# A transformer block on one core: both feed-forward products by seven block products in place of eight

## The chip, the core and the metric

The kernel runs on one core of one Trainium2 chip. The metric is device time in microseconds (us) of one execution; a time stated for a kernel is the median of its runs. Engines are named as the profile names them: PE is the matrix engine (PEld its weight loads), DVE the vector engine, ACT the scalar engine, POOL the GpSimd engine, SP the engine that issues most transfers. "L79" is line 79 of the kernel, the one helper through which almost every instruction of the four compute engines is recorded, so instructions are told apart by the tiles they write and read.

## What is computed

One block of a network on a sequence of 512 positions of width 2048, all in fp32: four token mixers on a joint projection, an output projection, and a feed-forward part with a squared ReLU. `N(v, w)` is `v * rsqrt(mean(v*v) + 1e-6) * w`.

```
h    = N(x, norm_mix_pre)
proj = h @ w_in                                    # 2048 x 6152
mix  = concat(hgrn2(..), gated_delta(..), spatial_gating(..), conformer_conv(..))
x    = x + N(mix @ w_out, norm_mix_post)           # 2048 x 2048
h    = N(x, norm_ff_pre)
y    = square(relu(h @ w_ff1)) @ w_ff2             # 2048 x 8192, 8192 x 2048
out  = x + N(y, norm_ff_post)
```

## The kernel before

**Precision.** The large products run in the `float32r` type. Each operand is split into a high part (`wh`, `xH`, `yH`) and the rest (`wl`, `xL`, `yL`), and a product is three matmuls into one PSUM bank: high with high, high with low, low with high (`mm3`, L405). Every matmul loads its own 128 x 128 stationary operand.

**Weights.** One stream (`Stream`, L355 and on) carries all weights in pieces of 512 KB. SP loads a piece into `raw` (three buffers, L365), ACT copies it to `wh`, DVE subtracts and writes `wl` (four buffers each). `plan` lists the pieces in the order in which PE uses them. A piece of `w_ff1` is 128 partitions of 4 KB in a row; a piece of `w_ff2` is two rows of 2 KB per partition.

**Order.** The program is written out for each engine by `Driver`: the main stream is a generator of matmuls, and tasks are woken by its estimate of time. Each engine's queue then runs in the order written, and an instruction that waits holds back those behind it. PSUM has two banks of kind `pj` and six of kind `mx`.

**Stages.** The projections and mixers run first; `out_job` (two halves of the tokens) multiplies by `w_out`, `x2_tail` adds the residual, stores it to DRAM (`x2d`) and writes the normalised rows, transposed and split, into the resident tile `R`. The feed-forward part follows. Its first products (`split_job`, L1477) take half of the tokens at a time, 256 columns per matmul, while the tails of the other half still run; `extras` has prepared two of its four blocks of weights early. Then eight rounds: eight blocks of 128 hidden features (`proj_F`, L413: stationary weights, all 512 tokens as columns), each squared after ReLU and split into `yH` and `yL` in SBUF (`relu2`); then `ff2_job`, which multiplies these by 1024 rows of `w_ff2` (stationary activations, 512 columns of weights) and adds the sum into `acc` in SBUF (`acc_add`). The last round (`ff2_last`) takes the tokens one group after the other for the last columns and finishes each group with `final`: row statistics, residual from `x2d`, four or five stores (L1613).

Of the kernel before, what the change touches and what calls it, by code (L numbers as in the profile page):

```python
# [12 lines left out]
F32 = mybir.dt.float32  # L13
# [55 lines left out]
class Eng:  # L69
    """An engine whose instructions also advance the driver's estimate of when it is free."""  # L70
# [51 lines left out]
class Driver:  # L122
    """Interleaves the instruction streams of many generators around one main stream of matmuls.

    A generator yields ("pe", banks) before matmuls that read what it has just computed, an Event to
    wait for it, or ("bg",) to go on only when the vector engine has nothing else to do.
    """
# [118 lines left out]
    def idle(self):  # L246
        """Nothing else to do: move on to the time at which some task is due."""
# [5 lines left out]
    def main(self, gen):  # L253
        """Run the main stream's generator, feeding tasks in between."""
# [32 lines left out]
def hybrid_trunk(ctx: ExitStack, tc: tile.TileContext, a, out):  # L287
# [117 lines left out]
    def mm3(o, aH, aL, bH, bL, first, last):  # L405
        T.matmul(out=o, lhsT=aH, rhs=bH, start=first, stop=False)
        yield PE0
        T.matmul(out=o, lhsT=aH, rhs=bL, start=False, stop=False)
        yield PE0
        T.matmul(out=o, lhsT=aL, rhs=bH, start=False, stop=last)  # L410
        yield PE0
# [947 lines left out]
    def x2_tail(t, yw, ss, evs, fin):  # L1359
# [33 lines left out]
        yield from to_R(t // 2, (t % 2) * P, yw, "mx", pre, hev[t])  # L1393

    hev = [[Event() for _ in range(4)] for _ in range(NT)]
# [47 lines left out]
    FB, SPLIT = 8, 4  # L1443
    NB = DFF // P // FB
    w1, w2 = a['w_ff1'], a['w_ff2']
    for b in range(NB):
        for j in range(FB):
            if b > 0 or j < 2 or j >= SPLIT:
                plan_F(w1, b * FB + j)
        for c in range(4):  # L1450
            plan.extend((rows2(w2, b * FB + 2 * i, c * 512), 2, 512) for i in range(FB // 2))

    extra = {}
    es_x = ExitStack()

    def extras():
        es_mix.close()
        px = es_x.enter_context(tc.tile_pool(name="px", bufs=1, reuse_waits="tile", side="right"))
        for e in range(2 * (SPLIT - 2)):
            j, kh = 2 + e // 2, e % 2  # L1460
            raw = p2.tile([P, 8, P], F32, tag="rawx", name="rawx", bufs=1)
            nc.sync.dma_start(out=raw, in_=w1[j, :, kh * 8:(kh + 1) * 8, :])
            drv.cur.time = drv.dma(1 << 19)
            yield ("bg",)
            h, l = (px.tile([P, 8, P], F32R, name=f"wx{e}{i}") for i in range(2))
            S.copy(out=h, in_=raw)
            V.tensor_tensor(out=l, in0=raw, in1=h.bitcast(F32), op=ALU.subtract)
            extra[j, kh] = (h, l, None)
            yield ("bg",)

    drv.main(out_job(0))
    exe = drv.spawn(extras())
    drv.main(out_job(1))

    heads = [Event() for _ in range(SPLIT)]

    def split_job():  # L1477
        yield exe
        yield ("pe", 2, "pj")
        bs = [Bank("pj") for _ in range(2)]  # L1480
        us = dict(extra)
        for hf in range(2):
            for j in range(SPLIT):
                if hf == 0 and j >= 2:
                    yield PE1
                    bs.append(Bank())
                for kh in range(2):
                    if hf == 0 and j < 2:
                        us[j, kh] = yield from st.get()
                    wh, wl, uid = us[j, kh]  # L1490
                    for kk in range(8):
                        k = kh * 8 + kk
                        for t in (2 * hf, 2 * hf + 1):
                            yield hev[t][k // 4]
                        yield from mm3(bs[j].t[:, hf * 256:(hf + 1) * 256], wh[:, kk, :], wl[:, kk, :],
                                       R[:, hf, 0, k, :], R[:, hf, 1, k, :], k == 0, k == KT - 1)
                    if hf == 1 and j < 2:
                        st.done(uid)
                if hf == 1:
                    heads[j].fire(drv.pe + 0.15, bs[j])  # L1500

    drv.main(split_job())
    es2.close()
    es_x.close()
    p3 = ctx.enter_context(tc.tile_pool(name="p3", bufs=1, reuse_waits="tile"))
    yH = p3.tile([P, FB, SEQ], F32R, name="yH")
    yL = p3.tile([P, FB, SEQ], F32R, name="yL")
    acc = p3.tile([P, NT, D], F32, name="acc")
    wfp = p3.tile([P, D], F32, name="wfp")
    yev = {}  # L1510

    def relu2(ev, j):
        yield ev
        r = p3.tile([P, 512], F32, tag="r", name="r", bufs=2)
        y2 = p3.tile([P, 512], F32, tag="y2", name="y2", bufs=2)
        S.activation(out=r, in_=ev.val.t, func=AF.Relu)
        ev.val.free()
        S.activation(out=y2, in_=r, func=AF.Square)
        yield PE0
        V.tensor_tensor(out=yH[:, j, :], in0=r, in1=r, op=ALU.mult)  # L1520
        V.tensor_tensor(out=yL[:, j, :], in0=y2, in1=yH[:, j, :].bitcast(F32), op=ALU.subtract)

    def ff2_mms(o, t, k, wh, wl):
        yh, yl = yH[:, k, t * P:(t + 1) * P], yL[:, k, t * P:(t + 1) * P]
# [211 lines left out]
```

## Time and profile before

| | us |
|---|---|
| median of 3 runs | 2278.02 |
| lowest and highest | 2276.43, 2278.62 |
| span of the profiled execution, first to last instruction | 2273.2 |

The page of the profile gives the busy time of each engine, the span in 40 slices, the chain of work that ended last, the costliest groups of instructions and the DMA issues. The trace behind it also answers for single stretches: the busy time of every engine, the granted clock of PE, the share of the 16 DMA engines' time that packets took, and GB/s. The share can come out a little over one, since packets on one engine overlap. Times of single PE instructions overlap as well, so the pace of PE is read from how many matmuls a piece of the chain holds.

### The profile page before, as it was taken

Reading aid. Unit: us, or ns where it says so; the run is one execution under the profiler, and the core shown is the slowest. Engines: PE = TensorE matmul, PEld = TensorE weight load, DVE = VectorE, ACT = ScalarE, POOL = GpSimd, SP = SyncE. Lnnn points to the kernel's source line nnn. Section 1 sums busy time; section 2 is a strip of 40 time slices with the busy share of each in tenths; the row PEclk is TensorE's granted clock in tenths of the full one; section 3 lists DMA queues with packets and bytes.
Section 4 is the critical chain, followed back from the end, with each engine's and each line's share of the span. In section 5 each row is a group of like instructions: output and inputs, shape, how many; then the busy total and the mean of one; then the engine's idle time right before and its main releaser. Section 6 shows DMA issues by size and latency. Waiting matters only on the chain.

```text
span 2273.2 us, 25758 instructions
## 1 busy us (share of the span) xinstructions
PE 2241.5 (99%) x10393; PEld 1848.3 (81%) x10393; DVE 1063.1 (47%) x1494; ACT 786.7 (35%) x1157; POOL 150.5 (7%) x186
## 2 busy tenths in 40 slices
PE   9899999999999999999999999999999999999998
PEld 7788888888888789888888888888888888888886
DVE  4656666877765764333333333333333333333335
ACT  6354444555554553212212212212212222322222
POOL 0231011211110000000000000000000000000013
PEclk9999999999999999999999999999999999999999
DMA  8232222222237772333332323333332333233334
GB/s 299 70 93 79 82 81 65 84 84 75 84 105 262 235 246 90 100 93 99 96 93 93 102 93 93 102 93 93 93 102 93 96 98 95 93 96 93 98 131 137
DMA packets 101750, 250.62 MB, mean 110 GB/s; under 512 B 8688, under 2 KB 11264, under 8 KB 100864
## 3 DMA queue, kind: packets, MB, share of 16 engines
q1 hardware_dynamic: 99184, 244.79, 34.0%
q10 hardware_dynamic: 2448, 4.20, 0.5%
q8 instruction: 81, 1.33, 0.2%
q14 instruction: 37, 0.30, 0.0%
HBM read 240.56 MB, written 8.40 MB: 110 GB/s over the span
## 4 chain that ended last, share of the span: by engine, by line
PE 90%; DMA 3%; DVE 3%; ACT 2%; issue 1%; POOL 1%; SPq 0%; DVEq 0%; ACTq 0%; POOLq 0%
PE pj L79 47%; PE mx L79 43%; DVE wl L79 1%; ACT wh L79 1%; DVE xT L79 1%; DMA raw<-in_w_cv_dram 0%; DMA rawx<-in_w_ff_dram 0%; ACT L79 0%; DMA rsd<-rs 0%; DMA wpost<-in_w_mix_post_dram 0%; DMA raw<-in_w_out_dram 0%; DMA x<-x2d 0%; DMA xT<-in_x_t_dram 0%; DMA rows<-in_rows_dram 0%; DMA xt<-in_x_dram 0%
## 5 line engine op out<-in xcount | busy, mean ns | idle before, releaser
L79 PE MATMUL pj<-R,wh 128*128 128x512 f32 (+1 forms) x3328 | 1033.1, 389 | 0.0
L79 DVE TENSOR_TENSOR wl<-raw,wh 128x1024 fp32r<-128x1024 f32 (+1 forms) x413 | 509.9, 1236 | 1025.1 <-ACT wh L79 1022.8
L79 ACT CAST wh<-raw 128x1024 fp32r<-128x1024 f32 (+1 forms) x413 | 430.5, 1044 | 896.3 <-PE mx L79 454.9
L79 PEld LDWEIGHTS pj<-R,wh 128*128 128x128 f32 x3328 | 618.4, 188 | 119.5
L79 PE MATMUL pj<-R,wl 128*128 128x512 f32 (+1 forms) x1664 | 646.8, 389 | 0.0
L79 PE MATMUL mx<-wh,yL 128*128 128x512 f32 (+1 forms) x1032 | 405.9, 393 | 0.5 <-DVE acc L79 0.5
L79 PE MATMUL mx<-wl,yH 128*128 128x512 f32 (+1 forms) x1032 | 405.9, 393 | 0.0
L79 PE MATMUL mx<-wh,yH 128*128 128x512 f32 (+1 forms) x1032 | 405.8, 393 | 0.0
L79 PEld LDWEIGHTS pj<-R,wl 128*128 128x128 f32 x1664 | 313.0, 188 | 59.2
L79 PE MATMUL mx<-wh,R 128*128 128x512 f32 x768 | 242.0, 395 | 6.9 <-ACT wh L79 6.9
L79 PEld LDWEIGHTS mx<-wh,yL 128*128 128x128 f32 x1032 | 193.4, 187 | 47.3 <-DVE acc L79 0.7
L79 PEld LDWEIGHTS mx<-wl,yH 128*128 128x128 f32 x1032 | 193.4, 187 | 47.1 <-DVE wl L79 0.5
L79 PEld LDWEIGHTS mx<-wh,yH 128*128 128x128 f32 x1032 | 193.4, 187 | 46.6
L79 PEld LDWEIGHTS mx<-wh,R 128*128 128x128 f32 x768 | 145.8, 190 | 37.6 <-ACT wh L79 7.3
L79 PE MATMUL mx<-wl,R 128*128 128x512 f32 x384 | 152.2, 396 | 2.3 <-DVE wl L79 1.5
L79 ACT ACTIVATE r<-pj 128x512 f32<-128x512 f32 x62 | 37.1, 598 | 278.6 <-PE pj L79 276.8
L79 POOL TENSOR_TENSOR acc<-acc,wfp 128x512 f32<-128x512 f32 x15 | 22.3, 1511 | 1376.7 <-ACT y L79 1376.7
L79 DVE TENSOR_TENSOR acc<-mx,acc 128x512 f32<-128x512 f32 (+1 forms) x113 | 77.6, 687 | 36.4 <-PE mx L79 35.6
L79 DVE SCALAR_TENSOR_TENSOR mix<-dy,cols,mix 128x512 f32<-128x512 f32 x120 | 92.5, 771 | 0.4
L79 PEld LDWEIGHTS mx<-wl,R 128*128 128x128 f32 x384 | 72.9, 190 | 18.8 <-DVE wl L79 4.0
L79 ACT ACT_TABLE_LOAD x54 | 69.3, 1283 | 7.2 <-DVE X L79 3.4
L79 DVE TENSOR_TENSOR yL<-y,yH 128x512 fp32r<-128x512 f32 x64 | 44.3, 692 | 4.5 <-ACT y L79 2.1
(248 smaller groups left out, 1142.6 us busy)
## 6 DMA issues: line engine op xcount, KB each, us to landing
raw<-in_w_ff_dram SPq DMA_DIRECT2D x252, 512.0 KB, 3.6
raw<-in_w_f_dram SPq DMA_DIRECT2D x80, 512.0 KB, 3.7
raw<-in_w_out_dram SPq DMA_DIRECT2D x64, 512.0 KB, 4.3
xt<-in_x_dram SPq DMA_DIRECT2D x8, 512.0 KB, 7.6
raw<-in_w_ai_dram SPq DMA_DIRECT2D x8, 512.0 KB, 4.4
x<-in_x_dram SPq DMA_DIRECT2D x16, 256.0 KB, 6.5
x2d<-x ACTq DMA_DIRECT2D x16, 256.0 KB, 3.9
out_dram<-x SPq DMA_DIRECT2D x15, 256.0 KB, 2.2
```

Source lines behind the costliest of these rows:

```text
L79: r = f(*args, **kw)
```

## The change

Both feed-forward products are cut into 2 x 2 blocks and computed by the seven products of Strassen's scheme in Winograd's form. For `h @ w_ff1`, the tokens are halved (256 and 256), the 2048 inputs (eight tiles of 128 each) and the hidden features (32 blocks of 128 each); a unit `u` is one pair of hidden blocks, 32 units. For `y @ w_ff2`, the units are eight rounds (four hidden blocks of each half, 512 rows) by two columns of 512 of each half, 16 units. A unit has products numbered 1 to 7, and three of them (2, 4, 3) go on in the bank of another (1, 7, 5).

- Sums of activations: `to_S` computes, for the second half of the tokens, the operands `S6`, `S7` and part of `R`; `s4_job` makes `S3`.
- Sums of weights: a buffer `X`, `V` (`raw`) or `W` is loaded by SP, and further blocks are added to it in place by transfers of POOL with `accum_op=ALU.add`. `X` holds one sum after the other: it is split for product 7, gets another block added, is split for 6, again for 4. `mill` splits the sums as the stream did (ACT, then DVE).
- Thirteen units (`HEAD`) have products 1 and 2, which need the first half of the tokens alone, computed ahead (`head_job`); the results go to DRAM (`stash`) and come back in `setup1`.
- Hidden activations: after products 6, 4 and 3 of a unit `evac1` forms the four blocks, applies ReLU and the square, forms the seven operands of the second scheme, splits them and stores both parts to DRAM (`ydr`, 0.92 MB each). `load_y` brings them back into the room of `R`, 1 MB for each round and product, in rows of 1 KB.
- The second product's results add up in five SBUF tiles (`accu`, `accg`, `accp`, `accc`, `accd`) in `evac2`; `final` works on them in place. The residual rows for it are loaded ahead.

```diff
-    FB, SPLIT = 8, 4
-    NB = DFF // P // FB
+    NU1, NU2, HEAD = 32, 16, 13
+    heads = [(u, p) for j in range(HEAD + 1) for u, p in ((j, 1), (j - 1, 2)) if 0 <= u < HEAD]
...
+    def unit_bufs(blk, head, xtag):
...
+            B["V", i] = Buf("V", [[b11, b12]] if head else [[b11], [b12]])
+            B["X", i] = Buf(xtag, [[b12, b22], [b11], [b21]])
+            B["W", i] = None if head else Buf("W", [[b21]])
+            B["Z", i] = Buf("W", [[b22]])
+        where = {1: ("V", 0), 5: ("V", 0 if head else 1), 7: ("X", 0), 6: ("X", 1), 4: ("X", 2), 2: ("W", 0), 3: ("Z", 0)}
...
+        late = [(u - 1, 4), (u - 1, 3)] if u else []
+        if head:
+            seq2 += [(u, 7), (u, 5)] + late + [(u, 6)]
+        else:
+            seq2 += [(u, 1), (u, 7)] + late + [(u, 5), (u, 2), (u, 6)]
...
+    def add_in(buf, stage, srcs):
+        for i, src in enumerate(srcs):
+            yield PE0
+            G.dma_start(out=buf.t, in_=src, accum_op=ALU.add)
...
+    def mill():
+        for j, (buf, stage) in enumerate(order):
+            i = base0 + j
+            yield st.room[i]
+            yield buf.ready[stage]
...
+            split((h, l), buf.t)
...
+            if stage + 1 < len(buf.stages):
+                drv.spawn(add_in(buf, stage + 1, buf.stages[stage + 1]), at=drv.cur.time)
+            else:
+                buf.free.fire(drv.cur.time)
...
-    drv.main(split_job())
...
+    drv.main(head_job())
+    drv.drain(tail + hdone)
     es2.close()
...
+    xr = ctx.enter_context(tc.tile_pool(name="xr", bufs=1, reuse_waits="tile"))
+    pools["X"], pools["W"] = (xr, "X", 2), (xr, "W", 2)
...
+    for tag in ("V", "X", "W"):
+        drv.spawn(loader(tag))
+    drv.spawn(mill())
...
+    def evac1(u, p, ev):
...
+        elif p == 6:
+            V.tensor_tensor(out=u2, in0=bt, in1=p1, op=ALU.add)
+            b.free()
+            V.tensor_tensor(out=yt[:, 2, :], in0=banks[u, 7][0].t[:, 0:256], in1=u2, op=ALU.add)
+            mid[u, 7].fire(drv.cur.time)
+            V.tensor_tensor(out=yt[:, 2, :], in0=banks[u, 5][0].t[:, 0:256], in1=yt[:, 2, :], op=ALU.subtract)
+            mid[u, 5].fire(drv.cur.time)
...
+            split((yh, yl), yt[:, 1:8, :])
+            for hl, y in ((0, yh), (1, yl)):
+                nc.sync.dma_start(out=ydr[u, hl], in_=y.rearrange("p a b -> p (a b)").bitcast(F32))
...
+    def load_y(b, p, guard):
+        yield guard
+        for u in range(4 * b, 4 * b + 4):
+            yield yfin[u]
...
+        for hl in range(2):
+            nc.sync.dma_start(out=dst[:, :, hl, :].bitcast(F32),
+                              in_=ydr[4 * b:4 * b + 4, hl, :, i * 256:(i + 1) * 256].rearrange("k p t -> p k t"))
...
+            if u == NU1 and p == 1:
+                es_x.close()
+                pr = ctx.enter_context(tc.tile_pool(name="pr", bufs=1, reuse_waits="tile", side="right"))
+                pools["X2"] = (pr, "X2", 2)
+                drv.spawn(loader("X2"))
...
+            T.matmul(out=o, lhsT=ah, rhs=wh[:, q, :], start=k == 0 and p in (1, 5, 6, 7), stop=False, skip_group_check=on)
```

Three places in the queues, as built. The first is SP's queue where the feed-forward part starts. Before, the loads of `w_ff1` (names `raw_...`) follow those of `w_out` without a break:

```order
L365 DMA raw_6674<-in_w_out_dram 128x2x512
L365 DMA raw_6693<-in_w_out_dram 128x2x512
L365 DMA raw_6710<-in_w_ff1_dram 128x1024
L365 DMA raw_6727<-in_w_ff1_dram 128x1024
L365 DMA raw_6744<-in_w_ff1_dram 128x1024
```

Now, SP's queue at the end of the products computed ahead (`hst` is the staging tile of their results):

```order
L365 DMA raw_7593<-in_w_ff1_dram 128x1024
L1637 DMA stash_5376<-hst_7525 128x512
L1637 DMA stash_5376<-hst_7597 128x512
L1637 DMA stash_5376<-hst_7659 128x512
L1637 DMA stash_5376<-hst_7717 128x512
L1587 DMA raw_7784<-in_w_ff1_dram 128x1024
L1587 DMA raw_7786<-in_w_ff1_dram 128x1024
L1587 DMA raw_7788<-in_w_ff1_dram 128x1024
L1587 DMA X_7790<-in_w_ff1_dram 128x1024
L1587 DMA X_7792<-in_w_ff1_dram 128x1024
L1587 DMA W_7794<-in_w_ff1_dram 128x1024
L1587 DMA W_7796<-in_w_ff1_dram 128x1024
```

What moved: the first load of the sums stands behind the store of the last result computed ahead, and the load of `X` that the next product needs is the fourth behind it.

The second place is POOL's queue. Before, between the row statistics of the `w_out` stage (`w2`) and the end of the kernel it holds only multiplications of results by `wfp`:

```order
L79 TENSOR_TENSOR w2_6840<-w2_6840,nhalf_81 128x1
L79 TENSOR_TENSOR w2_6852<-w2_6852,nhalf_81 128x1
L79 TENSOR_TENSOR acc_7346<-acc_7346,wfp_7347 128x512 x13
L79 TENSOR_TENSOR w1_15447<-w1_15447,nhalf_81 128x1
L79 TENSOR_TENSOR acc_7346<-acc_7346,wfp_7347 128x512
```

Now, from the same statistics on (all DMA rows here are accumulating ones):

```order
L79 TENSOR_TENSOR w2_6819<-w2_6819,nhalf_81 128x1
L79 TENSOR_TENSOR w2_6831<-w2_6831,nhalf_81 128x1
L79 DMA raw_7784<-in_w_ff1_dram 128x1024
L79 DMA raw_7786<-in_w_ff1_dram 128x1024
L79 DMA raw_7788<-in_w_ff1_dram 128x1024
L79 DMA X_7790<-in_w_ff1_dram 128x1024
L79 DMA X_7792<-in_w_ff1_dram 128x1024
L79 DMA X_7790<-in_w_ff1_dram 128x1024 x2
L79 DMA raw_7849<-in_w_ff1_dram 128x1024
L79 DMA X_7792<-in_w_ff1_dram 128x1024
```

What moved: 256 accumulating transfers of 512 KB each, in one order, stand where POOL was idle, and the first one for `X_7790` is behind three for `raw`.

The third place is SP's queue where the first product gives way to the second. Before, in the first round:

```order
L365 DMA raw_7245<-in_w_ff1_dram 128x1024
L1664 DMA wfp_7347<-in_w_ff_post_dram 128x2048
L365 DMA raw_7404<-in_w_ff1_dram 128x1024
L365 DMA raw_7439<-in_w_ff2_dram 128x2x512
L365 DMA raw_7471<-in_w_ff2_dram 128x2x512
```

Now, at the only such place (`R_85<-ydr` are activations coming back, `X2` the sum that product 7 of unit 32 needs):

```order
L1587 DMA raw_14304<-in_w_ff2_dram 128x2x512
L1587 DMA W_14333<-in_w_ff2_dram 128x2x512
L1783 DMA R_85<-ydr_5375 128x4x256 x8
L1587 DMA X2_14430<-in_w_ff2_dram 128x2x512
L1587 DMA X2_14432<-in_w_ff2_dram 128x2x512
L1758 DMA ydr_5375<-yh_14441 128x1792
L1758 DMA ydr_5375<-yl_14442 128x1792
L1587 DMA X_14512<-in_w_ff2_dram 128x2x512
```

What moved: the loads of `X2` stand behind eight loads of activations, the last of which wait for PE to be done with product 2 of unit 31.

## Rows read from the trace of the kernel before

**Rows 1.** The page: busy time of each engine over the span.

```profile
PE 2241.5 (99%) x10393; PEld 1848.3 (81%) x10393; DVE 1063.1 (47%) x1494; ACT 786.7 (35%) x1157; POOL 150.5 (7%) x186
```

**Rows 2.** The chain that ended last, feed-forward part: start us, us, what.

```profile
844.20 11.51 PE pj L79 x96
...
872.24 9.71 PE pj L79 x81
881.95 11.21 PE mx L79 x96
893.15 43.54 PE pj L79 x192
936.70 89.59 PE mx L79 x384
1026.29 87.05 PE pj L79 x384
1113.33 89.59 PE mx L79 x384
...
2086.13 87.05 PE pj L79 x384
```

**Rows 3.** Stretches: engines' busy us, then PE clock, DMA share, GB/s.

```profile
10.00:30.00 20.00, 20.00 (x88) 16.49 (x87) 11.57 (x19) 10.12 (x17) 0.22 (x1) 1.00 1.05 406
715.00:720.00 5.00, 5.00 (x24) 4.14 (x23) 2.45 (x2) 1.85 (x3) 0.00 (x0) 1.00 1.03 367
57.00:130.00 73.00, 66.09 (x303) 53.61 (x302) 46.95 (x81) 29.71 (x46) 18.79 (x12) 0.98 0.26 76
1026.29:2173.17 1146.88, 1146.88 (x4993) 936.52 (x4993) 393.07 (x416) 279.95 (x318) 0.00 (x0) 1.00 0.31 96
2263.90:2273.20 9.30, 0.00 (x0) 0.00 (x0) 5.29 (x8) 1.42 (x4) 3.08 (x4) 0.66 0.58 218
```

**Rows 4.** Who waited for whom from 893 to 2252 us: us, times, longest.

```profile
ACT wh L79 <- PE mx L79: 411.3, 93, 4.6
ACT r L79 <- PE pj L79: 276.8, 60, 4.6
ACT wh L79 <- PE pj L79: 189.8, 60, 4.2
```

**Rows 5.** Groups of instructions: count | busy us, mean ns of one | idle before.

```profile
L79 DVE TENSOR_TENSOR wl<-raw,wh 128x1024 fp32r<-128x1024 f32 x231 | 283.0, 1225 | 801.6 <-ACT wh L79 801.6
L79 ACT CAST wh<-raw 128x1024 fp32r<-128x1024 f32 x231 | 241.6, 1046 | 691.5 <-PE mx L79 374.3 <-PE pj L79 189.8 <-DVE acc L79 127.4
L79 DVE TENSOR_TENSOR acc<-mx,acc 128x512 f32<-128x512 f32 x96 | 66.4, 691 | 29.3 <-PE mx L79 28.7
L79 DVE TENSOR_TENSOR R<-mix,R 128x256 fp32r<-128x256 f32 x32 | 11.6, 418 | 1.7 <-ACT R L79 1.7
```

**Rows 6.** DMA issues, whole kernel: count, KB each, median us from issue to landing.

```profile
raw<-in_w_ff_dram SPq DMA_DIRECT2D x252, 512.0 KB, 3.6
raw<-in_w_cv_dram SPq DMA_DIRECT2D x7, 512.0 KB, 7.9
```

More of the change, by code (lines that the diff above doesn't have):

```diff
@@ new lines, in hybrid_trunk @@
+    seen = set()
+    for u, p in seq2:
+        for buf, stage in ub[u][p]:
+            order.append((buf, stage))
+            if id(buf) not in seen:
+                seen.add(id(buf))
+                rings[buf.tag].append(buf)
+    def add_in(buf, stage, srcs):
+        for i, src in enumerate(srcs):
+            yield PE0
+            G.dma_start(out=buf.t, in_=src, accum_op=ALU.add)
+            drv.cur.time = max(drv.dma(1 << 19), drv.cur.time + 2.5)
+        buf.ready[stage].fire(drv.cur.time)
@@ L1471, in hybrid_trunk @@
+    base0 = len(plan)
     drv.main(out_job(0))
-    exe = drv.spawn(extras())
+    open_px()
     drv.main(out_job(1))
[L1475 to L1500, printed above, removed]
@@ new lines, in hybrid_trunk, with head_mid, head_out @@
+    hmid = [Event() for _ in range(HEAD)]
+    hdone = [Event() for _ in range(HEAD)]
+    hst = {}
+    def head_mid(u, bank, ev):
+        yield ev
+        hst[u] = p2.tile([P, 512], F32, tag="hst", name="hst", bufs=2)
+        S.copy(out=hst[u][:, 0:256], in_=bank.t[:, 0:256])
+        hmid[u].fire(drv.cur.time)
+    def head_out(u, bank, ev):
+        yield ev
+        y = hst[u][:, 256:512]
+        S.activation(out=y, in_=bank.t[:, 0:256], func=AF.Relu)
+        bank.free()
+        S.activation(out=y, in_=y, func=AF.Square)
+        nc.sync.dma_start(out=stash[u], in_=hst[u])
+        hdone[u].fire(drv.cur.time)
@@ new lines, in soon, with head_job @@
+    def soon(t=0.15):
+        ev = Event()
+        ev.fire(drv.pe + t)
+        return ev
+    def head_job():
+        banks = {}
+        for u, p in heads:
+            if p == 1:
+                yield ("pe", 1, "pj")
+                banks[u] = Bank("pj")
+            else:
+                yield hmid[u]
+            wh, wl, uid = yield from st.get()
+            for k in range(8):
+                if u == 0:
+                    for t in range(2):
+                        yield hev[t][(k if p == 1 else 8 + k) // 4]
+                yield from mm1(banks[u], p, k, wh, wl, p == 1 and k == 0, k == 7, p == 2)
+            st.done(uid)
+            drv.spawn((head_mid if p == 1 else head_out)(u, banks[u], soon()))
@@ new lines, in hybrid_trunk, with setup1 @@
+    drv.spawn(s4_job())
+    yts, yset, yfin = {}, [Event() for _ in range(NU1)], [Event() for _ in range(NU1)]
+    mid = defaultdict(Event)
+    def setup1(u):
+        yield s4ev[1]
+        if u > 1:
+            yield yfin[u - 2]
+        yield PE0
+        yts[u] = p3.tile([P, 8, 256], F32, tag="yt", name="yt", bufs=2)
+        if u < HEAD:
+            yield hdone[u]
+            nc.sync.dma_start(out=yts[u][:, 3:5, :].rearrange("p a b -> p (a b)"),
+                              in_=stash[u])
+            drv.cur.time = drv.dma(1 << 18)
+        yset[u].fire(drv.cur.time)
@@ L1664, in hybrid_trunk @@
[L1664 to L1675 removed]
+        for c in range(4):
+            cs = slice(c * 512, (c + 1) * 512)
+            z = zev[t][c].val
+            if c == 1:
+                S.activation(out=z, in_=z, func=AF.Copy, scale=rs)
+                G.tensor_tensor(out=z, in0=x3[:, cs], in1=z, op=ALU.add)
+            else:
+                V.scalar_tensor_tensor(out=z, in0=z, scalar=rs, in1=x3[:, cs], op0=ALU.mult, op1=ALU.add)
```

516 lines of the change are left out of this document (343 added, 173 removed).

## Prediction

> **What bounds the kernel now.** I read the page's busy times first. PE is busy 99% of the span, and no other engine reaches half [rows 1]. Next the chain that ended last: from 844.20 us, where the first feed-forward matmuls start, its pieces are PE alone, one after the other [rows 2]. A piece of 384 matmuls of the first product takes 87.05 us, or 226.7 ns for one of 512 columns; one of the second product takes 89.59 us, or 233.3 ns. So the feed-forward part runs from 844.2 to 2263.9, 1419.7 us, and all that counts in it is the number and the width of matmuls. The stretches confirm it: from 1026 to 2173 us PE is busy without a gap at a granted clock of 1.00 (the 2.4 GHz level), DVE works 393 of 1147 us, ACT 280, POOL not at all, and the DMA engines have a share of 0.31 at 96 GB/s [rows 3]. The waits say who has room: ACT and DVE wait for PE to free buffers of weights, 411.3 and 189.8 us in all, never the other way for long [rows 4]. After the last matmul 9.3 us remain [rows 3]. The profiled span is 2273.2 us and the median 2278.02, so 4.8 us lie outside the span; I add them at the end.
>
> **The change part by part.**
>
> *Matmuls.* The first product had 3072 matmuls' worth of 512 columns; now 32 units of 7 products of 24 matmuls make 5376 of 256 columns. Their pace is not half of 226.7 (113.3 ns). The split job already runs this width: 96 in 11.51 us and 81 in 9.71 us, 119.9 ns each, and 96 in 11.21, 116.8 ns [rows 2]. I take 119.9, which two of three pieces show. The second product has 16 x 7 x 24 = 2688 matmuls of 512 columns, at 233.3 ns 627.1 us. The 26 products computed ahead are 624 matmuls, 74.8 us; the other 4752 take 569.8 us. PE alone now needs 1271.7 us where it had 1419.7: 148 us saved, 10.4% and not 12.5%, because of the narrow matmuls.
>
> *DVE and ACT.* A weight split costs DVE 1.225 us and ACT 1.046; an addition of 512 columns out of PSUM costs DVE 0.691, one of 256 columns 0.418 [rows 5]. A unit of the first product whose products 1 and 2 came from the stash has five splits (6.1), some nine additions of 256 columns (3.8), a copy and the split of seven blocks (2.1): about 12.3 us of DVE beside 5 x 24 x 0.1199 = 14.4 us of PE. A full unit has 14.5 beside 20.1. A unit of the second product has 14 splits and 14 additions, 17.2 + 9.7 = 26.8 beside 39.2. ACT has fewer. All of it is covered; in the first thirteen units by 2 us only, and what DVE needed beyond 14.4 us would count in full, thirteen times.
>
> *Transfers.* This is where the change can lose. Plain loads reach 406 GB/s with the DMA engines full, and 367 GB/s with the 2 KB rows of the second matrix [rows 3]. A stashed unit moves 3 loads of 0.52 MB, 1.84 MB of activations to DRAM and 0.26 MB of stash, 3.67 MB or 9.0 us, and 4 accumulating transfers; a full one 3.93 MB, 9.7 us, and 4; a unit of the second product 8 loads and 3.67 MB of activations, 7.86 MB or 21.4 us at 367, and 8. No row of before shows an accumulating transfer. Its lower bound is a plain pass, 0.524 MB / 406 = 1.29 us (1.43 at 367); its upper bound for occupancy two passes, 2.58 (2.86), if what stands in SBUF is read on the same path as what comes from DRAM. Between them I take 1.5 passes, since a plain pass moves each byte twice (one read, one write) and this one three times: 1.94 (2.14) us. Then:
> - a stashed unit needs 9.0 + 4 x 1.94 = 16.8 us beside 14.4 of PE. It is bound by transfers: +2.4, and I take 3 because the engines will not be full without a gap: 13 x 3 = 39 us;
> - a full unit 17.4 beside 20.1: hidden;
> - a unit of the second product 21.4 + 8 x 2.14 = 38.5 beside 39.2: just hidden, and I take +1 each for the same gaps, 16 us.
>
> *Waits added in queues.* SP's stores of hidden activations wait for their splits, and behind them in SP's queue stand the next units' loads. POOL runs its accumulates in one order, so a `V` sum of a later unit waits behind an `X` stage whose previous split is not done. Both act through the transfers above and are priced there and in the third rival.
>
> *Two seams.* Where the products computed ahead end, the `X` load for product 7 of unit 0 is the fourth load behind the last stash store, and its accumulate follows three on POOL. Four loads at 1.3 and a landing on top of 2.3 (the usual 3.6 us of a load [rows 6] less its own 1.3) are 7.5 us, the accumulate about 5.4 by the time its turn comes, the split 1.0 + 1.2: about 15 us in which PE has at most one product of `V`. I take 15.2, range 12 to 25. Where the first product gives way to the second, `X2` is loaded behind eight loads of activations, 0.5 MB each, that wait for PE: 10 us, range 0 (if `V` and `W` products cover it) to 18. After a stretch with gaps the granted clock is not at once 1.00: in 57 to 130 us, with PE busy 66 of 73 us, it is 0.98 [rows 3]. I add 3 us for both seams.
>
> *End.* The last unit's results are finished for all tokens at the end, not one group after the other: 12.5 us after the last matmul for 9.3.
>
> *Sum.* 844.2 + 74.8 + 15.2 + 569.8 + 39 + 13 + 627.1 + 16 + 12.5 = 2211.6 us, with the 4.8 outside the span **2216 us**.
>
> **The rivals.**
>
> *One: PE stays the bound.* If the accumulate costs little over a plain pass (1.29), a stashed unit needs 14.2 us of transfers beside 14.4, and a unit of the second product 32.9 beside 39.2. Then the 39 and the 16 go, and the seams shrink to 20 together: 844.2 + 74.8 + 569.8 + 627.1 + 12.5 + 20 + 4.8 = **2153 us** (2140 to 2175). For it: the DMA share of 0.31 leaves much room [rows 3]. Against: in thirteen units it needs the engines full without a gap.
>
> *Two, slower: the accumulate is two passes.* The DMA engines' read path takes both operands, so that each accumulate costs 2.58 (2.86) us. A stashed unit needs 9.0 + 10.3 = 19.4, +5.0, 65 us in all; a full unit 20.0 beside 20.1, about +1, 19 in all; a unit of the second product 21.4 + 22.9 = 44.3, +5.1, 82 in all. With 35 for seams and clock: 844.2 + 74.8 + 569.8 + 627.1 + 12.5 + 35 + 166 + 4.8 = **2334 us**. The point from which it decides: the kernel is slower than before once the accumulate costs about 2.4 us, 1.9 plain passes. For it: DRAM to SBUF at 406 GB/s with a share of 1.05 [rows 3] says that these engines have nothing left at the plain rate. Against: if the 406 are limited by writes, a second read costs less.
> The Trainium skill ("Collectives: The Full Stack", section "The bandwidth ceiling: the fold count and why AG ≠ RS ≠ AR") states this mechanism: an add needs two source reads, both on the same read ring, and a measured ratio to a copy of 1.93. By that ratio an accumulate would be 2.5 us and the kernel, as an estimate, about 2300; no run shown here has an accumulate, so I leave the sum on the rows.
>
> *Three: the chain through one buffer.* The transfers have room, but `X` is made in steps: a load, three accumulates, and after each accumulate a split of 2.3 us (1.05 + 1.23), one after the other, in two buffers, so that each chain must fit two units. At 3.6 us for each transfer [rows 6] the chain is 4 x 3.6 + 6.9 = 21.3, well within 28.8. At the landing time of a full queue, 7.9 us [rows 6], it is 38.5, or 19.2 for a unit beside 14.4: with 4.8 x 13 = 62 for the 39 it gives about **2240 us**; if an accumulate takes 12 us from issue to landing, 25.4 for a unit, about 2420. For it: issues in POOL's one order and waits ahead of SP's loads. Against: two buffers, and `V` and `W` products between.
>
> That the change does not do what it says I leave out: the built program has the 5376 and 2688 matmuls, 256 accumulating transfers and 64 stores of activations.
>
> **How the numbers follow.** The forecast (2185 to 2250) gets 0.35, rival one 0.22, rival two 0.28, rival three 0.15, half of it faster and half slower. About 0.2% is what a measurement of this kernel can tell from no change; the price of the accumulate would have to lie in a narrow band around 2.4 us for that: 0.04, taken from the neighbours' edges. Faster 0.62, slower 0.34. The range goes from 2145, the lower part of rival one, to 2345, past rival two; outside lie rival one's best and most of rival three's slow half, two in ten.
>
> **What would show it.** In the profile after, pieces of the chain at 119.9 and 233.3 ns a matmul confirm the PE terms; a DMA share near 1.0 in the stashed units, clearly under it in the full ones, confirms the transfer term, and GB/s there tell the passes. A PE idle time that ends on ACT's `wh`, and that in turn on a DMA, is rival two if the share is near 1.0, rival three if it is well under. Two single gaps of PE of 10 to 20 us are the seams. Wrong it would be above all if the second product's units last over 41 us, since sixteen of them weigh most.

## The result, and the profile after

The changed kernel takes 2422.66 us (median; 2412.11 to 2427.51) against 2278.31 before: a ratio of 1.0628, with a 95% interval from 1.0602 to 1.0655. It is slower by 6%, where 2216 was forecast, and it lies outside the range of 2145 to 2345. The profiled execution has a span of 2425.2 us.

The page after, with the lines that answer to [rows 1] and [rows 6]: busy time of each engine; the span in 40 slices (PE's busy tenths, its granted clock in tenths, the DMA engines' share in tenths); the two largest DMA queues (packets, MB, share of 16 engines: q1 is SP's, q0 POOL's); and DMA issues with the median from issue to landing.

```profile
PE 2155.4 (89%) x12097; PEld 1871.5 (77%) x12097; DVE 1452.8 (60%) x2028; ACT 1054.0 (43%) x1440; POOL 396.1 (16%) x428
...
PE   9999999999999985676779999998599999999895
...
PEclk9999999999999997888889999999799999999998
DMA  7222222222276656888889999999999999999994
...
q1 hardware_dynamic: 172864, 375.87, 44.4%
q0 software_dynamic: 53248, 134.23, 30.3%
...
X<-in_w_ff_dram POOLq DMA_DIRECT2D x192, 512.0 KB, 9.1
W<-in_w_ff_dram SPq DMA_DIRECT2D x115, 512.0 KB, 9.0
...
raw<-in_w_ff_dram POOLq DMA_DIRECT2D x64, 512.0 KB, 11.8
```

PE was busy 2241.5 us before and is busy 2155.4 now. There are more matmuls (12097 for 10393), since those of the first product are half as wide, but together they take less time. PE's share of the span fell from 99% to 89%, and the DMA engines, at 2 tenths in most of the slices ahead of `w_out`, stand at 8 and 9 in nearly all slices of the feed-forward part. POOL's 134 MB of accumulates hold the engines for 30.3% of the span, SP's 376 MB for 44.4%: byte for byte, an accumulate holds them nearly twice as long. Accumulates land after 9.1 and 11.8 us.

The same stretches as in [rows 3] (busy us of PE, PEld, DVE, ACT, POOL with instructions, then PE's clock, DMA share and GB/s): stashed units, full units, units of the second product.

```profile
1002.50:1268.90 266.40, 179.78 (x1335) 173.64 (x1334) 129.59 (x179) 91.41 (x89) 35.80 (x41) 0.84 0.88 235
1268.90:1686.40 417.50, 389.35 (x3161) 382.59 (x3162) 259.69 (x321) 215.28 (x249) 64.66 (x74) 0.99 1.00 274
...
1760.00:2300.00 540.00, 507.42 (x2139) 408.53 (x2139) 314.98 (x350) 188.65 (x189) 121.13 (x101) 0.97 1.09 288
```

Full units and the second product have PE at 93 and 94% with the DMA engines at 1.00 and 1.09: transfers set their pace, as [rows 3]'s 1.05 at 10 to 30 us looked. In the stashed units PE works two thirds of the time while the DMA engines are not full (0.88), and the clock falls to 0.84. Something besides the rate of transfers holds them. The waits from 1010 to 1250 us (us in all, times, longest) show what:

```profile
POOL X L79 <- DVE wl L79: 121.8, 14, 14.4
...
ACT wh L79 <- DMA X<-in_w_ff_dram: 72.3, 15, 10.4
...
PE mx L79 <- ACT wh L79: 69.9, 10, 14.7
...
POOL raw L79 <- DMA raw<-in_w_ff_dram: 53.8, 6, 13.1
```

From the third line upwards, and round again: PE waits for ACT's splits, ACT for an accumulate of `X` to land, POOL to issue the next accumulate until DVE's split of the sum before it is done. In [rows 4] ACT waited for PE. The chain that ended last has turned the same way. It was PE alone in [rows 2]; after, its longest pieces are landings of `X` in the first product and of `W` in the second:

```profile
1252.39 8.67 DMA X<-in_w_ff_dram
...
1827.60 28.29 DMA W<-in_w_ff_dram
```

The two seams, from PE's timeline (start, us, instruction; in brackets PE's idle time before it and what ended it):

```profile
966.95 0.80 PE L79 MATMUL mx<-S,wh 128*128 128x256 f32 x2 [26.50 <-ACT wh L79]
...
1722.63 0.79 PE L79 MATMUL mx<-wh,R 128*128 128x512 f32 x1 [29.69 <-ACT wh L79]
```

Against the terms of the forecast. A unit's period is read from the starts of its split of hidden activations (from unit 0 to 12, and 12 to 30), and in the second product from the loads of activations, 84.2 us for a round of two units. The seam's row holds what the others leave.

| term | forecast | measured | difference |
|---|---|---|---|
| products computed ahead, from 844.2 | 74.8 | 96.2 | +21 |
| first seam | 15.2 | 26.5 | +11 |
| 13 stashed units | 13 x 17.4 = 226 | 13 x 23.9 = 311 | +84 |
| 19 full units | 19 x 20.1 = 383 | 19 x 22.1 = 419 | +37 |
| second seam, with the clock | 13 | 38 | +25 |
| 16 units of the second product | 16 x 40.2 = 643 | 16 x 42.1 = 674 | +30 |
| after the last matmul | 12.5 | 16.8 | +4 |

Together 214 us, from 2211.6 to the span of 2425.2.

### The profile page after: what moved, and what is told of

It reads as the page before. It is cut to its first block, busy times and chain, and to the rows that moved or that the text cites. A ratio compares the mean times of both kernels' runs of the same rounds, so it can differ in the third digit from the quotient of the medians.

```text
span 2425.2 us, 31307 instructions
## 1 busy us (share of the span) xinstructions
PE 2155.4 (89%) x12097; PEld 1871.5 (77%) x12097; DVE 1452.8 (60%) x2028; ACT 1054.0 (43%) x1440; POOL 396.1 (16%) x428
## 3 DMA queue, kind: packets, MB, share of 16 engines
q1 hardware_dynamic: 172864, 375.87, 44.4%
q0 software_dynamic: 53248, 134.23, 30.3%
## 5 line engine op out<-in xcount | busy, mean ns | idle before, releaser
L79 PE MATMUL mx<-wh,R 128*128 128x512 f32 x2048 | 653.5, 397 | 55.1 <-ACT wh L79 50.7
L79 PE MATMUL pj<-R,wh 128*128 128x512 f32 (+1 forms) x2304 | 610.8, 350 | 14.0 <-ACT hst L79 14.0
L79 PEld LDWEIGHTS mx<-wh,R 128*128 128x128 f32 x2048 | 391.3, 191 | 143.3 <-ACT wh L79 55.9
L79 PEld LDWEIGHTS pj<-R,wh 128*128 128x128 f32 x2304 | 400.9, 191 | 61.0 <-ACT hst L79 16.0
L79 PE MATMUL mx<-wl,R 128*128 128x512 f32 x1024 | 406.9, 397 | 10.3 <-DVE wl L79 10.2
L79 DVE TENSOR_TENSOR wl<-X,wh 128x1024 fp32r<-128x1024 f32 x192 | 234.2, 1221 | 287.2 <-ACT wh L79 286.2
L79 PE MATMUL pj<-R,wl 128*128 128x512 f32 (+1 forms) x1152 | 402.0, 349 | 0.0
L79 PE MATMUL mx<-S,wh 128*128 128x256 f32 x1536 | 297.6, 294 | 109.7 <-ACT wh L79 109.7
L79 PEld LDWEIGHTS mx<-S,wh 128*128 128x128 f32 x1536 | 251.3, 201 | 113.4 <-ACT wh L79 113.4
L79 PE MATMUL mx<-S,wl 128*128 128x256 f32 x768 | 227.7, 296 | 14.5 <-DVE wl L79 14.4
L79 PEld LDWEIGHTS mx<-wl,R 128*128 128x128 f32 x1024 | 195.9, 191 | 57.2 <-DVE wl L79 16.7
## 6 DMA issues: line engine op xcount, KB each, us to landing
raw<-in_w_ff_dram POOLq DMA_DIRECT2D x64, 512.0 KB, 11.8
```

What stands on the lines that cost most here:

```text
L79: r = f(*args, **kw)
```

## The experiments

Two theories. **A**: the accumulate is dear; it holds the DMA engines for about two plain passes (the second rival). **B**: its occupancy is small, but each step of `X`'s chain waits for a landing (the third rival). Where no interval is given, a kernel was timed once; the four times of the changed kernel lie within 16 us.

**The price by itself** (`price`). Stages of 512 KB transfers without the block's work, by SP (`S`) and by POOL (`G`), with rows of 4 KB or (`two`) of 2 KB, and additions in SBUF at the end:

```diff
+    loads(S, 48)                              # A
...
+    loads(G, 48)                              # B
...
+    loads(G, 48, accum_op=ALU.add)            # C
...
+    loads(S, 48, two=True)                    # D
...
+    loads(G, 48, two=True, accum_op=ALU.add)  # E
...
+    for i in range(12):                       # G: one at a time, accumulating
+        G.dma_start(out=bufs[0], in_=s1(), accum_op=ALU.add)
...
+    for i in range(40):                       # H: one plain load beside one accumulate
+        S.dma_start(out=other[i % NBUF], in_=s1())
+        G.dma_start(out=bufs[i % NBUF], in_=s1(), accum_op=ALU.add)
```

> This kernel computes nothing of the block: it moves 512 KB blocks of the two feed-forward matrices into SBUF in stages, one after the other: 48 plain loads by SP's queue, 48 plain loads by POOL's, 48 accumulating ones by POOL's, the same two of the second matrix (2 KB rows), 12 plain and 12 accumulating ones each waiting for the last, 40 of either kind side by side, and at the end additions of 128 x 1024 on POOL and DVE, apart and side by side. Theory A (the price of the accumulate: it occupies the DMA engines for more than two plain passes): 48 plain loads take about 62 us, 48 accumulating ones 125 to 140 us (2.6 to 2.9 us each), 40 pairs 155 to 170 us. Theory B (the accumulate costs little more than a plain pass; what hurt was the chain of X, each step waiting for a landing): 48 accumulating ones take 62 to 80 us, and only those one at a time are slow (5 us or more each). An addition of 128 x 1024 on POOL: 3.0 us, by the 1.5 us of one of half the size.

Stretches within the stages A to E and H, in that order (busy us of DVE and POOL, then clock, DMA share, GB/s), and three accumulates that go one at a time:

```profile
10.00:66.00 56.00, 0.00 (x0) 1.56 (x9) 1.00 1.00 401
74.00:124.00 50.00, 0.00 (x0) 20.42 (x39) 1.00 1.03 407
145.00:240.00 95.00, 0.00 (x0) 32.35 (x39) 1.00 1.06 211
270.00:330.00 60.00, 0.00 (x0) 1.11 (x6) 1.00 1.05 385
340.00:420.00 80.00, 0.00 (x0) 40.97 (x35) 1.00 1.13 205
590.00:720.00 130.00, 0.00 (x0) 29.66 (x36) 1.00 1.05 275
```

```profile
518.18 0.84 POOL L340 DMA_DIRECT2D b<-in_w_ff_dram  x1 [4.91 <-DMA b<-in_w_ff_dram]
523.84 0.85 POOL L340 DMA_DIRECT2D b<-in_w_ff_dram  x1 [4.82 <-DMA b<-in_w_ff_dram]
529.55 0.84 POOL L340 DMA_DIRECT2D b<-in_w_ff_dram  x1 [4.85 <-DMA b<-in_w_ff_dram]
```

A plain transfer takes 0.524 MB / 407 GB/s = 1.29 us, from POOL's queue as from SP's (401 GB/s); an accumulate 0.524 MB / 211 GB/s = 2.49 us, 1.93 plain passes; with 2 KB rows 1.36 and 2.56. The share is 1.00 or more in all these stages, so the engines are full. A plain load and an accumulate side by side take 3.81 us (1.049 MB / 275 GB/s), which is the sum of the two prices: neither hides behind the other. One at a time an accumulate takes 5.7 us. POOL's queue is not what makes it dear; the accumulate is. That is theory A, though 48 accumulates at 2.49 make 120 us, a little under the 125 to 140 that were expected, and 1.93 passes are not more than two.

**No accumulates** (`plain`).

```diff
-            G.dma_start(out=buf.t, in_=src, accum_op=ALU.add)
+            G.dma_start(out=buf.t, in_=src)
```

> The 256 accumulating transfers become plain ones of the same size, queue and waits, so the sums are left out. Theory A: a full unit falls from 22.0 to 20.1 us, a unit of the second product from 42.1 to 39.2, a stashed one from 24.9 to 15 to 17, in all about 2422 - 110 - 36 - 46 = 2230 us, less some at the seams. Theory B: the chain of X keeps its four landings and three splits; stashed units stay over 20 us, the whole at 2330 or more.

This kernel leaves out the sums and keeps the transfers' sizes, queue and waits. 2266.91 us, 156 under the changed kernel, and between the totals that A and B expected. Stashed units, full units, second product:

```profile
992.60:1219.20 226.60, 175.55 (x1328) 168.74 (x1327) 129.33 (x179) 90.73 (x89) 21.73 (x41) 0.92 0.79 276
1219.20:1577.60 358.40, 357.11 (x2993) 356.49 (x2994) 245.76 (x304) 202.71 (x236) 38.13 (x72) 1.00 0.87 303
...
1660.00:2200.00 540.00, 539.80 (x2382) 446.65 (x2381) 358.25 (x395) 215.54 (x216) 80.45 (x113) 1.00 0.90 321
```

In the last two PE has next to no gap: 20.0 and 38.1 us a unit. There the price alone was the loss, as A has it. A stashed unit still takes 20.4 us at a share of 0.79, as B has it: with plain transfers, too, the chain is too long for two buffers. Neither theory alone gives 2267.

**A third buffer for the chain** (`x3`).

```diff
-    pools["X"], pools["W"] = (xr, "X", 2), (xr, "W", 2)
+    pools["X"], pools["W"] = (xr, "X", 3), (xr, "W", 2)
```

> X gets three buffers for two in the first product. Theory A: full units stay at 22.0 us with the DMA share at 1.00, stashed ones fall to 20.6 at best (9.0 + 4 x 2.9), units of the second product unchanged: 2370 to 2420 us. Theory B: stashed units fall to 15 to 17 and full ones to 20.1: about 2270 us.

2360.6 us, 62 less. Stashed units fall from 23.9 to 18.8 us, and now at full engines; full units stay at 22.0 (22.1 before):

```profile
1005.80:1231.80 226.00, 190.26 (x1416) 185.22 (x1416) 138.83 (x189) 100.87 (x100) 37.16 (x44) 0.89 1.03 290
1261.60:1607.60 346.00, 328.20 (x2690) 324.10 (x2689) 220.51 (x272) 179.66 (x209) 56.10 (x64) 0.99 1.00 280
```

So the rivals are not alternatives: the chain cost 5 us a stashed unit on top of the price. That 18.8 comes so near to 9.0 + 4 x 2.49 = 19.0 is in part luck: POOL issued 44 accumulates in this stretch of twelve units, not 48.

**Both at once** (`plainx3`): the two edits above together.

> Both suspects taken away at once: plain transfers in place of the 256 accumulating ones (the sums are left out) and three buffers for X. With plain transfers alone a stashed unit still took 20.6 us on average at a DMA share of 0.79; with three buffers alone 18.8 at 1.03, which is transfers. If the two causes are the price of the accumulate and the chain through X's two buffers, and nothing else holds a stashed unit: 14.4 to 15.5 us here, and the whole 12 x 5.5 = 65 us under plain's 2267, about 2200. If DVE's or ACT's queue holds them too: 17 or more, and no more than 45 us under it.

2218.41 us. Stashed units take 16.5, 3.9 less than with plain transfers alone, and full ones run without a gap:

```profile
1000.00:1170.00 170.00, 155.29 (x1209) 152.28 (x1209) 117.31 (x161) 83.93 (x82) 18.46 (x35) 0.94 0.91 335
1200.00:1540.00 340.00, 340.00 (x2858) 340.00 (x2857) 233.02 (x290) 190.54 (x222) 36.11 (x68) 1.00 0.88 302
```

Price and chain account for 7.4 of the 9.5 us that a stashed unit lies over its matmuls. The other 2.1 us were not traced further, and 16.5 lies between the two outcomes expected. PE's gaps at the seams are left, with 22.2 and 20.8 us: this kernel lies 65 us over the first rival, whose price it has.

**Products computed ahead** (`hst3`).

```diff
-        hst[u] = p2.tile([P, 512], F32, tag="hst", name="hst", bufs=2)
+        hst[u] = p2.tile([P, 512], F32, tag="hst", name="hst", bufs=3)
```

> The staging tile of the products computed ahead gets three buffers for two. By the trace ACT waited 19.4 us there for stores of the stash, and these 26 products took 97 us for 75 of matmuls. If that wait is the cause, they take 80 us or less and the whole falls by 15 to 20 us, to about 2405 us; if the cover of other work (weights that come late, the tails of the stage ahead) sets the pace, nothing changes. Theories A and B expect the same of the units behind.

2411.25 us, 11 less, which the total alone could not tell from the spread of the changed kernel's runs. Read in the stage itself, the products ahead take 86 us for 96; the first gap stays (26.60 us). So about half of that term, 10 of 21 us, was ACT waiting for a staging tile whose store had not landed.

**Additions on DVE in place of accumulates.** Some blocks that a sum needs are in SBUF anyway. Six kernels use them.

`vadd`: in full units and in the second product `X` gets `V` added, and `V`'s own accumulate then has to wait for that; in stashed units `V` gets `Z` added and carries the sums of 6 and 4.

```diff
-            B["V", i] = Buf("V", [[b11, b12]] if head else [[b11], [b12]])
-            B["X", i] = Buf(xtag, [[b12, b22], [b11], [b21]])
+            B["V", i] = Buf("V", [[b11, b12], B["Z", i], [b21]] if head else [[b11], [b12]])
+            B["X", i] = Buf(xtag, [[b12, b22]] if head else [[b12, b22], B["V", i], [b21]])
...
+                if isinstance(more, Buf):
+                    V.tensor_tensor(out=buf.t, in0=buf.t, in1=more.t, op=ALU.add)
```

> One accumulate of four in every unit becomes an addition on DVE of a block that SBUF holds already: in full units and in the second product X gets V added (before V's own accumulate), in stashed units V takes over the sums for products 6 and 4 and gets Z added, so that X has one accumulate only and V two. If the price measured alone (2.49 us each) and the chain through X are what made the kernel slow: a stashed unit falls from 24.9 (with its neighbours 22.2 on average) to 16.3 to 18, a full one from 22.0 to 20.3, a unit of the second product from 42.1 to 38.5 to 39; in all about 2250 us (2235 to 2290). If DVE becomes the bound instead (13.5 us of work beside 14.4 of PE in a stashed unit, in one queue with waits), stashed units stay over 20 and the whole over 2300 us.

2346.85 us: stashed units 19.8, the second product at PE's pace (38.1 a unit), but full units 23.2, worse than 22.1, with the DMA engines no longer full:

```profile
1237.30:1635.40 398.10, 362.02 (x2858) 350.74 (x2857) 250.60 (x306) 190.59 (x222) 44.03 (x51) 0.98 0.85 235
```

That is neither of the two outcomes expected. DVE is busy 63% there, so it is not short of time. ACT's timeline in one unit shows a wait that fits:

```profile
1402.28 1.05 ACT L79 CAST wh<-W 128x1024 fp32r<-128x1024 f32 x1
1409.23 1.04 ACT L79 CAST wh<-raw 128x1024 fp32r<-128x1024 f32 x1 [5.90 <-DMA raw<-in_w_ff_dram]
```

`V`'s accumulate now starts only after product 7's split and must land before product 5's, two products later; ACT stands 5.9 us for it here, and 5.8 on average the 13 times that it does so between 1237 and 1550 us. In the second product, where a product takes twice as long, units of the same order run at PE's pace. That this wait is the cause was not tested by moving it alone.

`v2` adds edits at the seams: 10 units ahead, a third staging tile, `V`'s loads started while the products ahead run, the free `X` buffers for the first unit of the second product with the last unit's 4 and 3 ahead of its 7, and a dearer accumulate in the planner.

```diff
+                if self.nd == len(plan) and self.hook is not None:
+                    self.hook()
...
+    st.hook = lambda: drv.spawn(loader("V"))
...
+        elif u == NU1:
+            seq2 += [(u, 1)] + late + [(u, 7), (u, 5), (u, 2), (u, 6)]
```

> As the last, and the seams: 10 units computed ahead for 13, three staging tiles for their results, the sums of V loaded while the products ahead still run (and the first unit's X in V's buffers), the first unit of the second product with its X in the buffers that are free, and products 4 and 3 of the last unit ahead of its product 7; the planner counts an accumulate as two loads. If the rest of the loss sits in the two seams (26 and 30 us) and in the products ahead (22 us over their matmuls): 60 us under the last, about 2180 us (2160 to 2210), faster than the kernel before by 4%. If the clock or other waits take the seams' place, no more than 20 us under the last.

2330.40 us, a ratio of 1.0232 (1.0215 to 1.0249): 16 under `vadd`, where 60 were expected, which is the second outcome. The sums started earlier (the first product of sums at 933.7 us), but full units got no better (23.5), and at the second seam a gap of 25.29 us remained.

`v3` takes other sums for DVE: `Z` into `X` for product 7 and `W` into `X` for product 4; `V`'s accumulate is back in its place, and the first unit of the second product does 5 and 2 ahead of 7.

```diff
+                B["X", i] = Buf(xtag, [[b12] if one else [b12, b22], [b11], B["W", i]])
+                B["X", i].pre = B["Z", i] if one else None
...
+    pools["X"], pools["W"], pools["Z"] = (xr, "X", 2), (xr, "W", 1), (xr, "Z", 2)
```

> As v2, but with other additions on DVE: full units keep V's accumulate as it was, and X gets Z added (for product 7) and W (for product 4), both loaded ahead, so that a full unit has two accumulates and no landing of an accumulate stands between two products next to each other; the second product's X gets W added (six accumulates for eight), V as in the changed kernel. The first unit of the second product does 5 and 2 ahead of 7. If full units of v2 and vadd (24 us at a DMA share of 0.83) were held by the landing of V's accumulate between products 7 and 5, they fall to 20.2 to 20.8 us here, units of the second product from 39.8 to 38.3, and the whole to about 2330 - 22 x 3.5 - 24 - 15 = 2215 us (2200 to 2240), under the kernel before by 2.5%. If they were held by DVE's queue (15.7 us of work there, 17.0 here beside 20.1), they stay at 23 or more and the whole over 2290.

2440.56 us, a ratio of 1.0712 (1.0695 to 1.0730). With only two accumulates a unit, full units took 24.0 us, and the total is over 2290, which is the second outcome:

```profile
1150.00:1580.00 430.00, 391.03 (x3011) 383.69 (x3010) 285.92 (x340) 203.01 (x234) 31.09 (x36) 0.94 0.69 208
```

A share of 0.69 and DVE at 66%: no engine is full, and PE's granted clock is 0.94 on average. The timelines of DVE and ACT at the end of one unit:

```profile
1323.42 1.22 DVE L79 TENSOR_TENSOR X<-X,Z 128x1024 f32<-128x1024 f32 x1
1324.55 1.34 DVE L79 TENSOR_TENSOR yt<-mx,yt 128x256 f32<-128x256 f32 x3
```

```profile
1324.73 0.37 ACT L79 COPY yt<-pj 128x256 f32<-128x256 f32 x1 [3.28 <-PE pj L79]
1325.00 2.00 ACT L79 CAST wh<-X 128x1024 fp32r<-128x1024 f32 x2
```

The addition of `Z` stands in DVE's queue right ahead of the evacuations of product 6 and of the split that PE waits for; ACT waits 3.28 us for PE's product 1 ahead of the same split. That reading was not tested by moving this addition alone. In the second product `Z`'s two pieces had to go through one buffer, and units took 47 us; that the buffer is the reason was not tested alone either.

`v4` keeps only additions with slack on both sides: `W` into `X` after product 6's split in full units (three accumulates), `V` into `X` in the second product (as `vadd`), `X` in three buffers, and `v3`'s seams with the planner's prices as they were.

```diff
+            if one and not head:
+                B["X", i].stages[2] = B["W", i]
+            elif not one and not first2:
+                B["X", i].stages[1] = B["V", i]
...
+    pools["X"], pools["W"], pools["Z"] = (xr, "X", 3), (xr, "W", 1), (xr, "Z", 1)
```

> The changed kernel with: X in three buffers in the first product; product 4's sum in full units by an addition of W on DVE (three accumulates a unit); in the second product X gets V added on DVE (six accumulates for eight); 10 units computed ahead for 13 and the two seams as in v2, with 5 and 2 ahead of 7 in the first unit of the second product. v3 showed full units at 24 us with a DMA share of 0.69 and the clock at 0.94: transfers had room there, and ACT and DVE sat behind evacuations in their queues. If what v3 lost came from the additions that stood right ahead of a split (Z into X) and from the second product's single buffer for Z: stashed units 18.8, full ones 20.3 to 21, units of the second product 39.8, the whole about 2225 us (2205 to 2250). If any addition in DVE's queue costs PE its lead and so its clock: full units 23 or more, 2290 or more.

2257.29 us, a ratio of 0.9906 (0.9890 to 0.9923): 0.9% faster than the kernel before, though 32 us over what was expected and outside that range. Stashed units, full units, second product:

```profile
971.20:1121.00 149.80, 126.23 (x975) 122.74 (x976) 94.03 (x128) 66.49 (x64) 26.07 (x30) 0.93 1.04 296
1130.00:1550.00 420.00, 415.87 (x3460) 413.05 (x3459) 306.68 (x373) 231.66 (x269) 53.95 (x62) 1.00 0.94 272
...
1630.00:2180.00 550.00, 544.03 (x2383) 448.11 (x2381) 393.09 (x424) 214.18 (x217) 100.53 (x84) 1.00 1.03 284
```

Full units 20.4 and the second product 38.1 us: PE is the bound again. The stashed units (18.8) are full of transfers (1.04), and the seams still have gaps: 12.5 and 7.8 us at the first, 16.7 and 7.2 at the second. Since `v4` has a third buffer for `X` as well, it does not show by itself which of the two made its full units faster than `vadd`'s.

`adds` is `v4` without the edits at the seams and with 13 units ahead.

> v4's additions and its three buffers for X and for the staging tile, but 13 units ahead and both seams as in the changed kernel. If the seams' edits are worth what they moved (first product of sums 20 to 25 us earlier, a gap of 7 us for 30 at the second), this takes 2254 + 45 = about 2300 us; if the additions alone carry v4, 2265 or less.

2278.96 us: 22 over `v4`, half of what was expected. Its units run like `v4`'s (18.7, 20.6, 38.1), so the additions and the third buffers carry some 144 of the 165 us between the changed kernel and `v4`, the seams 22. The third buffers alone were worth 62 and 11 us (`x3`, `hst3`); if that adds up, some 70 are the additions'.

`v5` makes the stashed units of `v4` like full ones (`W` loaded and added on DVE); against `v4`:

```diff
...
-            if one and not head:
+            if one:
...
```

> As v4, with stashed units made like full ones: W is loaded for them too and added to X on DVE for product 4, so that they have three accumulates for four (one more plain load). v4's stashed units took 19 to 21 us at a DMA share of 1.02. If transfers hold them, they fall by 2.5 - 1.3 = 1.2 us of transfers at least, to about 18 us, and the whole by 15 to 30 us, to 2225 to 2243. If DVE holds them (13.5 us beside 14.4), no change or slower.

2246.89 us, a ratio of 0.9866 (0.9849 to 0.9882), the fastest of those that compute the block. The gain is 10 us and not 15 to 30. Stashed units take 18.3 for 18.8, which is 4 of the 10; the DMA engines are still full there.

```profile
966.80:1113.00 146.20, 127.26 (x974) 123.13 (x972) 101.13 (x133) 66.78 (x65) 18.12 (x21) 0.94 1.01 304
```

## Why the prediction was wrong

**The bound before, and the matmul terms: right.** 4752 matmuls at 119.9 ns were forecast; where nothing held PE, 2858 took 340.00 us, 119.0 ns (`plainx3`). The second product was even mis-sized to its own disadvantage: at 233.3 ns [rows 2] a unit would take 39.2 us, but `plain` ran 2382 matmuls in 540 us, 226.7 ns, so that its floor is 38.1. Why they were slower before was not traced.

**The price of the accumulate: the first step that failed.** The forecast put it between one and two plain passes and took 1.5 "since a plain pass moves each byte twice (one read, one write) and this one three times". Measured alone it is 1.93 passes, 2.49 us for 1.94. The reason given counts bytes moved; what fills up is the engines' time, and of that the second operand takes nearly as much as the first. No row of before held an accumulate, so the 1.5 was a choice; the one row that bore on it, 406 GB/s at a share of 1.05 [rows 3], spoke for the second rival.
The Trainium skill's rule ("Collectives: The Full Stack", section "The bandwidth ceiling: the fold count and why AG ≠ RS ≠ AR"), which the prediction set aside to stay on its rows, names a measured ratio of 1.93 between a collective that copies and one that adds. 407 / 211 GB/s here agrees.

**The price is not enough.** Put into the forecast's own sum, 2.49 and 2.56 us make 19.0 us of a stashed unit (+20 in all) and 41.9 of a unit of the second product (+27): 2263 us, or 2287 with the gaps that the forecast allowed for: about the time of the kernel before, and inside the range. The rest of the miss has other steps.

**The chain, left out of the sum: the second step.** The waits of `X`'s chain were priced in the third rival alone, and the forecast's sum has nothing for them. The second rival gave 2334 us and the third 2240; they were weighed as separate cases, each with the other's term left at its forecast. But a dearer transfer is also a later landing: the accumulates of `X` took 9.1 us to land in the median, where one alone takes 5.7 from issue to issue, and the chain of four transfers and three splits lengthens with them. `x3` takes away the chain and leaves 18.8 us a stashed unit, close to the second rival's 19.4; the chain adds 5.1, close to the 4.8 of the third. In the stashed units the sum of both, 19.0 + 4.8, is what the kernel did (23.9): 84 us over the forecast. The third rival's slow half names about 2420 us, next to the 2423 measured, but that is luck: by its own terms 25.4 us a unit gives 2216 - 39 + 13 x 11 = 2320.

**Full units: hidden, said the forecast, and were not.** 17.4 us of transfers were set beside 20.1. With 2.49 for 1.94 that is 19.6, still hidden; measured were 22.1 at a share of 1.00, and 20.0 without accumulates (`plain`). The queues of that stretch, 1268.9 to 1686.4 us (packets, MB, share of 16 engines):

```profile
q0 software_dynamic: 10588, 38.53, 50.1%
q1 hardware_dynamic: 18518, 75.43, 49.6%
```

The trace has the size of each packet, and with it what each kind of transfer held of the 16 engines' time: an accumulate 2.82 us, a plain load 1.43, and the stores of a unit (packets of 7168 B) 5.0 us where 4.5 had been counted. 4 x 2.82 + 4 x 1.43 + 5.0 = 22.0. All three are more than the sum had for them. Part of that is how a share counts: accumulates by themselves stood at 1.06, so that their 2.49 us are 2.6 of packets. The rest was not traced. In `plain` the same count gives 1.44, 1.53 and 5.2, so the stores' price hardly depends on the accumulates.

**The second product: mechanism right, size off.** 38.5 us of transfers were forecast beside PE; 42.1 came, at a share of 1.09, and 38.1 without accumulates (`plain`). Eight accumulates at 2.56 for 2.14 are 3.4 us of the difference. The forecast named units over 41 us as the main sign of being wrong; they came, but with 30 us they weigh less than the stashed units.

**The seams and the products ahead.** The gaps stood where they were expected, at 26.5 and 29.7 us for 15.2 and 10. The first was within 2 us of its range's end; the second had the loads of `X2` behind activations' loads, as said. The dear transfers explain only part of it: with plain ones and a third buffer 22.2 and 20.8 us stay (`plainx3`), and why these are longer than forecast was not traced. What the forecast did not have is that the products ahead would not run at PE's pace: 96 for 75 us, half of it the staging tile with two buffers, whose reuse waits for a store to land. Of a moved step I had counted the matmuls and the store's bytes, not the time until its buffer is free again.

Two readings in the prediction were off without weight in the result: both waits that it gives to ACT and DVE, 411.3 and 189.8 us, are ACT's [rows 4], and what lies outside the span is 1.8 us in the profiled execution after (2426.95 for 2425.2), not 4.8.

## What to carry to other kernels

Price a transfer that adds as two transfers until a trace says otherwise, and give it its latency too where sums are made step by step: count the buffers in such a chain against landing times at full engines, not idle ones. Rivals that do not exclude each other add up; work out the case in which all of them hold. When work moves from an idle-looking unit to another, look at what stands next to it in the queue: an addition of 1.2 us on DVE went with a gain where both its sides had slack (`v4`, which has a third buffer too), and with a loss in full units where it stood right ahead of the split that PE waits for, or ahead of a landing (`v3`, `vadd`). The timelines say so; no run moved one addition alone.

## What the runs showed of the hardware

- An accumulating transfer of 512 KB from DRAM into SBUF takes 2.49 us of full DMA engines against 1.29 for a plain one, 3.81 for one of each side by side, and 5.7 us from issue to issue when it goes alone. Issued plain, POOL's queue is as fast as SP's (407 and 401 GB/s).
- In `v3`'s full units gaps cost PE twice. It was busy 391 of 430 us, at a mean granted clock of 0.94; without gaps (`plain`) it stood at 1.00, the 2.4 GHz level. The stretch of 430 us held 17.9 units, 358 us of work by the 20.0 of `plain`: beside 39 us of gaps the matmuls took 33 us longer, of which the clock makes some 26 (430 x 0.06, an estimate).
- Additions of 128 x 1024 in SBUF took 2.33 us on POOL (`price`) and 1.22 on DVE (`v3`), but in `price`, where both engines added at once, eight on DVE took 31.5 us, 3.9 each. The additions therefore went to DVE alone.
